# Output projection of a hybrid decoder layer: half of its feature tiles by seven half-size products for eight

## The chip, the cores and the metric

One core of a Trainium2 chip runs the whole layer. The metric is the device time of one execution in microseconds, the median of several runs; a profile is one such execution, and its rows are read with times counted from the start of its span.

## What is computed

A decoder layer on 512 tokens of 2048 features, in fp32. RMS-normed input times a combined weight gives queries, keys, values, gates and gate paths (z) of two head groups: an attention group of 16 heads (NSA, with a branch over compressed blocks of keys and values) and a recurrent group of 8 heads (HGRN2). The parts that matter here:

```python
kc = compress_blocks(k_cmp, pe_k, w1_k, w2_k)      # gelu(blk @ w1) @ w2
vc = compress_blocks(v_cmp, pe_v, w1_v, w2_v)      # the second compression
...
o_a = head_rmsnorm(o_a, nsa_out_norm[l], NSA_HEADS) * jax.nn.silu(z_a)
o_h = head_rmsnorm(o_h, hgrn_out_norm[l], HGRN_HEADS) * jax.nn.silu(z_h)
mixed = jnp.concatenate([o_a, o_h], axis=-1)       # (512, 2048)
x = x + mixed @ w_out[l]                           # w_out: (2048, 2048)
return rmsnorm(x, final_norm)
```

## The kernel before

**Matmuls.** Every large product is done in two-part numbers. An operand is cast to the fp32r type (the high part, on ScalarE) and the rest is subtracted out (the low part, on VectorE); `parts` does so for weights (L315, L316), `split` for transposed activations (L215, L216). A product of 128 features, 128 tokens and 512 columns is then three TensorE matmuls: high by high, low by high, high by low. Weights come by DMA from SyncE's queue (SP) as 128x1024 pieces; the raw piece and its two parts are three of the ten buffers of the pool `w` (`WBUF`).

**Order.** The stages are Python generators; `run` interleaves two of them by the costs that they yield, which gives the order of the program. A list scheduler then lays out each engine's queue: earlier in the program goes first, but what its plan takes to be ready may go ahead. Each engine then works its queue strictly in that order.

**The stages.** First the keys and values to be compressed, then projections of which 12 of 16 feature tiles are already done by seven half-size products for eight (`seven`). Then key and query projections (`make_kd`, `make_q`; 48 matmuls each, L571 to L573) beside the two compressions (`compress`): the first beside query pair 1, the second beside `make_kd(0, 1)` and `make_q(2)`. `blocks` (L623 to L637) builds a compression's input from rows that DMAs bring back, for the second one on GpSimd's queue. The compression's first product is L653 (two passes for each fp32 matmul), its last L682. Then `attention`, interleaved with the remaining key and query projections as filler; then the recurrent heads with further projections as filler.

**Gating.** `gate_chunk(zc, ...)` normalizes four tiles of heads, multiplies by the gate path (L1146, VectorE), transposes on TensorE into the bank `ps_tp` (L1136; there is one such bank) and splits the result (L215 on ScalarE, L216 on VectorE) into the left operand `mT`. Chunks 0 and 1 (attention heads) give feature tiles 0 to 7, chunks 2 and 3 (recurrent heads) tiles 8 to 15. `z_proj` makes the gate paths on TensorE; chunks 1 and 2 run beside its last call.

**Output projection.** Three column chunks of 512 go through `proj_tm` (L596 to L598): for each pair of feature tiles the weights, then four token tiles. Chunk 3 of the gating runs beside the first of them. At the end of a chunk `out_done` adds the residual on VectorE (L1219), squares on ScalarE (L1221) and multiplies by the final norm's gain on GpSimd (L1222). The last column chunk (`last_chunk`, weights loaded ahead by `last_weights`) goes token tile by token tile (L1248 to L1250), so that each finished row can be normalized (L1251 to L1272) and written while the next is multiplied.

**Left over from `seven`:** the list `free_banks` of PSUM bank pairs. When it has been used for the two projections by `seven`, it stands at (lp, lp), (tp, ot), (pj, pj), (pj, pj).

## Time and profile before

| | us |
|---|---|
| median of 3 runs | 1099.39 (1098.72 to 1101.68) |
| the profiled execution | 1101.15 |
| its span in the profile | 1099.4 |
| TensorE busy in it | 1077.6 (98%), mean granted clock 0.995 |
| VectorE busy | 658.2 (60%) |
| ScalarE busy | 419.7 (38%) |
| GpSimd busy | 98.6 (9%) |

PE is TensorE, PEld its weight loads, DVE VectorE, ACT ScalarE, POOL GpSimd, SP SyncE. Matmuls are pipelined: a matmul's time is longer than the distance to the next one's start, and it is the distance that counts for the sum. On VectorE, too, an instruction can start a little before the one ahead of it has ended. The chain of waits is followed back from the last instruction; "busy" says nothing of whether an engine was waited for. A line such as L316 stands for every call of the helper.

### The profile page before, as it was taken

What the parts mean: (1) busy time and instruction counts of PE and PEld (TensorE: products, weight loads), DVE (VectorE), ACT (ScalarE), POOL (GpSimd) and SP (SyncE); (2) the same over time, 40 slices, a digit from 0 to 9 for tenths busy, and PEclk for the clock granted to TensorE, in tenths of its full rate; (3) what the DMA queues carried; (4) which work ended last, traced back from release to release, by engine and by line L of the source; (5) the groups of instructions that cost most, each with busy time, mean ns of one, the idle gap of its engine ahead of it and who ended that gap; (6) DMA issues with size and microseconds to landing.
All of it is one profiled execution on the core that took longest, in us unless ns stands there. A gap on an engine that the chain in (4) does not pass through costs nothing.

```text
span 1099.4 us, 15321 instructions
## 1 busy us (share of the span) xinstructions
PE 1077.6 (98%) x5644; PEld 888.2 (81%) x5644; DVE 658.2 (60%) x1550; ACT 419.7 (38%) x835; POOL 98.6 (9%) x170
## 2 busy tenths in 40 slices
PE   9999999999989999999999999999999999999996
PEld 8799888888868777777877888888887888888886
DVE  4767756764444676576765565666676788424332
ACT  6534433442123565555553222222222443324211
POOL 1000000102431020110200000000000000202010
PEclk9999999999999999999999999999999999999999
DMA  9535346544973322222212323221221723334223
GB/s 311 167 104 172 106 139 212 158 161 140 278 203 96 77 58 58 62 73 58 59 39 78 95 69 106 77 77 58 77 74 48 249 91 106 111 112 167 100 86 125
DMA packets 100011, 127.46 MB, mean 116 GB/s; under 512 B 6672, under 2 KB 62368, under 8 KB 99936
## 3 DMA queue, kind: packets, MB, share of 16 engines
q1 hardware_dynamic: 94368, 113.90, 33.9%
q0 software_dynamic: 2624, 8.39, 2.2%
q10 hardware_dynamic: 2944, 4.19, 1.1%
q8 instruction: 45, 0.74, 0.3%
q14 instruction: 30, 0.25, 0.1%
HBM read 106.01 MB, written 12.06 MB: 107 GB/s over the span
## 4 chain that ended last, share of the span: by engine, by line
PE 91%; DVE 4%; issue 2%; DMA 2%; ACT 1%; SPq 0%; ACTq 0%; POOL 0%; DVEq 0%; POOLq 0%
PE pj L571 9%; PE pj L572 9%; PE pj L573 9%; PE pj L596 7%; PE pj L598 7%; PE pj L597 7%; PE ot L838 4%; PE pj L819 3%; PE lp L987 3%; PE pj L470 2%; PE pj L468 2%; PE pj L469 2%; PE lp L805 2%; PE lp L653 2%; PE lp L806 1%
## 5 line engine op out<-in xcount | busy, mean ns | idle before, releaser
L316 DVE TENSOR_TENSOR w<-w,w 128x1024 fp32r<-128x1024 f32 (+3 forms) x169 | 204.0, 1213 | 180.7 <-ACT w L315 89.3
L315 ACT CAST w<-w 128x1024 fp32r<-128x1024 f32 (+3 forms) x169 | 173.0, 1036 | 273.2 <-DMA w<-in_w_in_dram 150.5
L571 PE MATMUL pj<-hh,w 128*128 128x512 f32 x448 | 183.5, 410 | 0.7 <-ACT pt L828 0.7
L572 PE MATMUL pj<-hl,w 128*128 128x512 f32 x448 | 178.4, 398 | 0.0
L573 PE MATMUL pj<-hh,w 128*128 128x512 f32 x448 | 176.5, 394 | 0.0
L596 PE MATMUL pj<-w,hh 128*128 128x512 f32 (+2 forms) x352 | 127.1, 361 | 0.0
L597 PE MATMUL pj<-w,hl 128*128 128x512 f32 (+2 forms) x352 | 125.9, 358 | 0.0
L598 PE MATMUL pj<-w,hh 128*128 128x512 f32 (+2 forms) x352 | 125.6, 357 | 0.0
L571 PEld LDWEIGHTS pj<-hh,w 128*128 128x128 f32 x448 | 84.3, 188 | 18.5 <-issue 2.9
L573 PEld LDWEIGHTS pj<-hh,w 128*128 128x128 f32 x448 | 84.2, 188 | 17.3 <-issue 0.3
L572 PEld LDWEIGHTS pj<-hl,w 128*128 128x128 f32 x448 | 84.4, 188 | 16.7 <-issue 2.1
L774 DVE CUSTOM_DVE_ANT_0 s<-s,lp 128x128 f32<-128x128 f32 (+3 forms) x128 | 60.5, 483 | 38.4 <-PE lp L806 35.4
L779 ACT ACTIVATE s<-s,mn 128x128 f32<-128x128 f32 (+3 forms) x128 | 71.6, 560 | 28.4 <-DVE mn L774 19.1
L598 PEld LDWEIGHTS pj<-w,hh 128*128 128x128 f32 x352 | 66.4, 189 | 8.5
L596 PEld LDWEIGHTS pj<-w,hh 128*128 128x128 f32 x352 | 66.5, 189 | 8.2
L597 PEld LDWEIGHTS pj<-w,hl 128*128 128x128 f32 x352 | 66.5, 189 | 7.9
L819 PE MATMUL pj<-ident,s 128*128 128x128 f32 x320 | 53.8, 274 | 0.4 <-ACT s L779 0.4
L828 ACT COPY pt<-pj 128x256 f32<-128x256 f32 (+2 forms) x56 | 25.7, 458 | 57.7 <-PE pj L819 57.5
L838 PE MATMUL ot<-pt,s 128*64 128x512 f32 (+3 forms) x256 | 47.3, 440 | 0.0
L819 PEld LDWEIGHTS pj<-ident,s 128*128 128x128 f32 x320 | 39.7, 140 | 9.5 <-ACT s L779 3.0
L838 PEld LDWEIGHTS ot<-pt,s 128*64 128x64 f32 x256 | 22.9, 136 | 21.5 <-issue 11.8
L596 PE MATMUL pj<-w,s 128*128 128x512 f32 x96 | 37.7, 393 | 0.0
(349 smaller groups left out, 1926.2 us busy)
## 6 DMA issues: line engine op xcount, KB each, us to landing
w<-in_w_in_dram SPq DMA_DIRECT2D x121, 512.0 KB, 3.6
w<-in_w_out_dram SPq DMA_DIRECT2D x32, 512.0 KB, 3.5
s<-s SPq DMA_DIRECT2D x48, 128.0 KB, 2.3
w<-in_x_dram SPq DMA_DIRECT2D x16, 256.0 KB, 6.6
d<-e POOLq DMA_DIRECT2D x12, 256.0 KB, 2.4
l<-in_x_dram SPq DMA_DIRECT2D x12, 256.0 KB, 5.2
out_dram<-l SPq DMA_DIRECT2D x12, 256.0 KB, 3.1
w<-in_w_in_dram SPq DMA_DIRECT2D x5, 456.0 KB, 3.2
```

What stands on the lines that cost most here:

```text
L315: nc.scalar.copy(hi, raw)
L316: nc.vector.tensor_tensor(lo, raw, hi.bitcast(FP32), ALU.subtract)
L571: nc.tensor.matmul(acc[j], wh, hh, start=kk == 0, stop=False)
L572: nc.tensor.matmul(acc[j], wh, hl, start=False, stop=False)
L573: nc.tensor.matmul(acc[j], wl, hh, start=False, stop=kk == NK - 1)
L596: nc.tensor.matmul(o, ah, hi[:, k, :], start=kk == 0, stop=False)
L597: nc.tensor.matmul(o, al, hi[:, k, :], start=False, stop=False)
L598: nc.tensor.matmul(o, ah, lo[:, k, :], start=False, stop=kk == NK - 1)
L774: nc.vector.tensor_tensor_reduce(out=y, in0=e["bias"][:, 384 - i * P:512], in1=lp, scale=1.0, scalar=3e38, op0=ALU.add, op1=ALU.min, accum ...
L779: nc.scalar.activation(y, y, AF.Exp, bias=mn, scale=-1.0, accum_out=e["ls"][:, 2 * i + b:2 * i + b + 1])
L819: nc.tensor.transpose(tps[:, j * P:(j + 1) * P], y[:, j * P:(j + 1) * P], ident)
L838: nc.tensor.matmul(e["ot"][b * 64:(b + 1) * 64, j * P:512], v_tok[j][:, b * 256 + g * DH:b * 256 + (g + 1) * DH], e["pt"][:, b, j * 512:38 ...
```

## The change

The output projection is done in two halves of 1024 columns (`out_pair`). In each, feature tiles 0 to 7 (four pairs) are multiplied by a seven-product scheme: the left operand is cut into blocks of 256 tokens by 128 features (A11, A12, A21, A22) and sums of them (S1 to S4), the weights likewise into two blocks of columns and sums of these (`first`, `second`, `third`); two pairs of feature tiles make one step. Tiles 8 to 15 are multiplied as before (`left_out`), into the same banks. The left sums are made by `y_sums` after gating chunk 1, into 12 tiles of the pool `late`, which grows to 21. Corrections from the products go through VectorE (`after_first`, `after_third`) into u2 and u3; GpSimd adds them to the residual (`take_room`), and VectorE adds the bank to that (`out_done`). The first step's products use the bank pairs (lp, lp), (tp, ot) and (pj, pj) in the order A11, S3, S2. In the last column block, tiles 8 to 15 go row by row as before, with their weights kept ready.

The second compression runs beside `make_kd(1, 0)`, which was the first filler of the attention stage; `make_kd(0, 1)` and `make_q(2)` go ahead of it without it.

```diff
--- before.py
+++ after.py
-NLATE = 18
+NLATE = 21
...
+    ysum = []
+    def y_sums(lo, hi):
+        for j in range(lo, hi):
+            pr = [[mT[part][2 * j + r] for part in range(2)] for r in range(2)]
+            a = b4(FP32).rearrange("p (r c) -> p r c", r=2)
+            for r in range(2):
+                nc.vector.tensor_tensor(a[:, r], pr[r][0].bitcast(FP32), pr[r][1].bitcast(FP32), ALU.add)
+            x11, x21, x12, x22 = [a[:, r, h * 256:(h + 1) * 256] for r in range(2) for h in range(2)]
+            t = sl()
+            nc.vector.tensor_tensor(t[:, 0:256], x21, x11, ALU.subtract)
+            nc.vector.tensor_tensor(x22, x21, x22, ALU.add)
+            nc.vector.tensor_tensor(x11, x11, x22, ALU.subtract)
+            nc.vector.tensor_tensor(x12, x12, x11, ALU.add)
+            d2, d14 = late(F32R), [late(F32R), late(F32R)]
+            d2 = [d2[:, 0:256], d2[:, 256:512]]
+            d3 = [pr[0][part][:, 256:512] for part in range(2)]
+            for (h, l), src in ((d3, t[:, 0:256]), (d2, x11), (d14, a[:, 1])):
+                nc.scalar.copy(h, src)
+                nc.vector.tensor_tensor(l, src, h.bitcast(FP32), ALU.subtract)
+            ysum.append({"S2": d2, "S4": [d[:, 0:256] for d in d14], "S1": [d[:, 256:512] for d in d14], "S3": d3,
...
+            yield 0.5
...
-        run((chain(make_kd(0, 1), make_q(2)), 22), (compress(vblk, w1_v, w2_v, False), 22))
-    fill = [make_kd(1, 0), make_q(3), make_kd(1, 1)] + [make_q(p) for p in range(4, 8)]
+        run((chain(make_kd(0, 1), make_q(2)), 22))
+        run((make_kd(1, 0), 11), (compress(vblk, w1_v, w2_v, False), 10))
+    fill = [make_q(3), make_kd(1, 1)] + [make_q(p) for p in range(4, 8)]
...
-        run((attention(), 160), (chain(*fill, hgrn_qf(0)), 113))
+        run((attention(), 160), (chain(*fill, hgrn_qf(0)), 102))
...
-        (chain(gate_chunk(1, o_nsa[4:8], 2, sz[1]), gate_chunk(2, o_h[0:4], 1, sz[2])), 21))
+        (chain(gate_chunk(1, o_nsa[4:8], 2, sz[1]), y_sums(0, 4), gate_chunk(2, o_h[0:4], 1, sz[2])), 23))
...
+    PO = 4
+    wo_half = w_out2.rearrange("(j h p) c -> h p j c", h=2, p=P)
...
+    def take_room(t, c, alloc, u=None):
+        y = alloc()
+        nc.sync.dma_start(out=y, in_=x2[t * P:(t + 1) * P, c * 512:(c + 1) * 512])
+        if u is not None:
+            nc.gpsimd.tensor_tensor(y, y, u, ALU.add)
+        ys[t][c] = y
+    def out_done(t, c, bank):
+        y = ys[t][c]
+        add(y, y, bank)
+        junk = sl()
+        nc.scalar.activation(junk, y, AF.Square, accum_out=yss[:, t, c:c + 1])
+        nc.gpsimd.tensor_tensor(y, y, fns[c], ALU.mult)
+    def left_out(bank, t, k0, w, cs=slice(0, 512)):
+        hi, lo = w
+        for k in range(2):
+            ah, al = [mT[part][k0 + k][:, t * P:(t + 1) * P] for part in range(2)]
...
+    def out_pair(p):
+        c0 = 1024 * p
+        last = p == 1
+        t2 = b8("hl3").rearrange("p (g j c) -> p g j c", g=2, j=2)
...
+        def products(jj, left, bank, fresh, w):
+            hi, lo = w
+            if fresh and jj == 0:
+                banks[bank] = free_banks.pop(0)
+                acc[bank] = [f() for f in banks[bank]]
+            for tt in range(2):
+                ts = slice(tt * P, (tt + 1) * P)
+                for j in range(2):
+                    ah, al = [v[:, ts] for v in ysum[2 * jj + j][left]]
...
+        def first(jj):
+            b11, b22, b12 = load(0, jj, 0), load(1, jj, 1), load(0, jj, 1)
+            w1 = parts(b11)
+            sub(b12, b12, b22)
+            sub(t2[:, jj], b12, b11)
+            return w1, parts(b12), parts(t2[:, jj])
+        def second(jj):
+            b21, t4 = load(1, jj, 0), b4(FP32).rearrange("p (j c) -> p j c", j=2)
+            add(t4, t2[:, jj], b21)
+            return parts(t4), parts(b21)
+        def third(jj):
+            b22 = load(1, jj, 1)
+            add(t2[:, jj], t2[:, jj], b22)
+            return parts(t2[:, jj]), parts(b22)
+        alloc = (lambda: late()) if p == 0 else (lambda: sl())
+        def after_first():
+            u2.extend([sl(), sl()])
+            u3.extend([sl(), sl()])
+            for tt in range(2):
+                nc.scalar.copy(u2[tt], acc["1"][tt])
+            for tt in range(2):
+                add(u2[tt], acc["6"][tt], u2[tt])
+                add(u3[tt], acc["7"][tt], u2[tt])
+            free_banks.extend([banks["6"], banks["7"]])
+            for t in range(NT):
+                take_room(t, 2 * p, late, u3[t - 2] if t > 1 else None)
+        def after_left():
+            for t in range(NT):
+                out_done(t, 2 * p, acc["14"[t // 2]][t % 2])
+            free_banks.extend([banks["4"], banks["1"]])
+            for tt in range(2):
+                take_room(2 + tt, 2 * p + 1, alloc, u3[tt])
+        def after_third():
+            for tt in range(2):
+                add(u2[tt], acc["5"][tt], u2[tt])
+                take_room(tt, 2 * p + 1, alloc, u2[tt])
...
+        for prepare, names, after in (
+                (first, (("A11", "1", True), ("S3", "7", True), ("S2", "6", True)), after_first),
+                (second, (("A22", "4", True), ("A12", "1", False)), None),
+                (third, (("S1", "5", True), ("S4", "3", True)), after_third)):
...
+                    if right and last:
+                        v = b8(("hh2", "hl2", "hh3", "hl3")[n], F32R)
+                        to = v[:, 0:1024], v[:, 1024:2048]
+                    return load_w(w_out2, k0, 2, c0 + 512 * right, 512, to)
...
+        for n in range(len(steps) + 1):
+            if n < len(steps):
+                while steps[n][4] > len(mT[0]):
+                    yield None
+                ready.append(steps[n][0]())
...
-    last_w = []
-    for c in range(3):
...
-        p = proj_tm([], w_out2, mT, c * 512, 512, out_done(c))
-        if c == 0:
-            run((p, 41), (gate_chunk(3, o_h[4:8], 1, sz[3]), 17))
...
-    last_chunk()
+    run((out_pair(0), 82), (gate_chunk(3, o_h[4:8], 1, sz[3]), 42))
+    run((out_pair(1), 1))
```

## Rows read from the trace of the kernel before

**Rows 1.** Chain of waits, shares of the span by engine.
```profile
PE 91%; DVE 4%; issue 2%; DMA 2%; ACT 1%; SPq 0%; ACTq 0%; POOL 0%; DVEq 0%; POOLq 0%
```

**Rows 2.** Windows: length; busy us of PE, PEld, DVE, ACT, POOL; clock; DMA.
```profile
340.00:660.00 320.00, 317.36 (x1733) 246.50 (x1732) 204.13 (x605) 154.31 (x400) 34.02 (x60) 1.00 0.26 71
859.00:942.00 83.00, 82.48 (x394) 67.16 (x393) 71.66 (x212) 35.16 (x50) 0.00 (x0) 1.00 0.39 125
959.00:1045.00 86.00, 86.00 (x381) 71.23 (x380) 30.39 (x32) 26.47 (x36) 10.98 (x9) 1.00 0.39 132
```

**Rows 3.** Timeline of TensorE, 296 to 350 us: start, us, instruction, [idle before].
```profile
299.77 1.95 PE L653 MATMUL lp<-s,w 128*128 128x128 f32 x16
301.47 0.48 PE L571 MATMUL pj<-hh,w 128*128 128x512 f32 x1
...
327.11 10.30 PE L653 MATMUL lp<-s,w 128*128 128x128 f32 x64 [5.36 <-issue]
337.16 0.47 PE L571 MATMUL pj<-hh,w 128*128 128x512 f32 x1
...
348.74 0.39 PE L573 MATMUL pj<-hh,w 128*128 128x512 f32 x1
```

**Rows 4.** Windows of TensorE: length, busy, granted clock, DMA.
```profile
330.00:331.00 1.00, 1.00 (x7) 0.50 0.00 0
```

**Rows 5.** Timeline of ScalarE, then of VectorE, 258 to 350 us.
```profile
310.26 1.05 ACT L315 CAST w<-w 128x1024 fp32r<-128x1024 f32 x1
322.57 1.04 ACT L315 CAST w<-w 128x1024 fp32r<-128x1024 f32 x1 [11.26 <-DMA w<-in_w_in_dram]
...
324.79 3.83 DVE L637 TENSOR_TENSOR s<-s,col 128x124 f32<-128x124 f32 x14
```

**Rows 6.** Timeline of TensorE in the output projection.
```profile
911.83 0.39 PE L596 MATMUL pj<-w,s 128*128 128x512 f32 x1
...
912.64 0.48 PE L598 MATMUL pj<-w,s 128*128 128x512 f32 x1
...
958.76 0.39 PE L596 MATMUL pj<-w,s 128*128 128x512 f32 x1
...
959.45 0.39 PE L596 MATMUL pj<-w,s 128*128 128x512 f32 x1
```

**Rows 7.** Timeline of VectorE from 835 to 962 us.
```profile
845.12 0.42 DVE L966 TENSOR_TENSOR s<-s,s 128x256 f32<-128x256 f32 x1 [1.22 <-PE tp L1032]
...
903.77 0.69 DVE L1158 SCALAR_TENSOR_TENSOR s<-s,pj 128x512 f32<-128x512 f32 x1
904.37 0.17 DVE L143 TENSOR_SCALAR roi<-roa 128x16 int32<-128x16 int32 x1
...
907.46 1.23 DVE L316 TENSOR_TENSOR w<-w,w 128x1024 fp32r<-128x1024 f32 x1
908.60 0.17 DVE L151 TENSOR_TENSOR roi<-roi,rot 128x16 f32<-128x16 f32 x1
...
953.22 1.49 DVE L316 TENSOR_TENSOR w<-w,w 128x1024 fp32r<-128x1024 f32 x1 [1.73 <-ACT w L315]
```

**Rows 8.** Groups of VectorE, 859 to 942 us: count, busy, mean ns, idle before.
```profile
L316 DVE TENSOR_TENSOR w<-w,w 128x1024 fp32r<-128x1024 f32 x13 | 15.9, 1222 | 0.6 <-ACT w L315 0.6
...
L216 DVE SCALAR_TENSOR_TENSOR hl<-tp,col,hh 128x512 fp32r<-128x512 f32 x8 | 6.0, 750 | 5.6 <-ACT hh L215 5.5
```

**Rows 9.** Groups of GpSimd over the whole span.
```profile
L1222 POOL TENSOR_TENSOR l<-l,s 128x512 f32<-128x512 f32 x12 | 17.9, 1495 | 199.6 <-ACT s L1221 199.6
```

**Rows 10.** Timeline of VectorE, 1040 to 1100 us.
```profile
1078.64 0.69 DVE L1251 TENSOR_TENSOR s<-s,pj 128x512 f32<-128x512 f32 x1 [6.10 <-PE pj L1250]
...
1082.62 0.75 DVE L1268 SCALAR_TENSOR_TENSOR s<-s,la,s 128x512 f32<-128x512 f32 x1
```

**Rows 11.** Timeline of ScalarE, 930 to 950 us.
```profile
933.48 0.69 ACT L215 ACTIVATE hh<-tp,col 128x512 fp32r<-128x512 f32 x1 [4.32 <-PE tp L1136]
...
938.05 0.69 ACT L215 ACTIVATE hh<-tp,col 128x512 fp32r<-128x512 f32 x1 [2.95 <-PE tp L1136]
```

More of the change, by code (lines that the diff above doesn't have):

```diff
@@ L1213, in hymba_layer @@
     fns = []
-    def out_done(c):
-        def done(t, acc):
-            y = late()
-            nc.sync.dma_start(out=y, in_=x2[t * P:(t + 1) * P, c * 512:(c + 1) * 512])
-            nc.vector.tensor_tensor(y, y, acc, ALU.add)
-            junk = sl()
-            nc.scalar.activation(junk, y, AF.Square, accum_out=yss[:, t, c:c + 1])
-            nc.gpsimd.tensor_tensor(y, y, fns[c], ALU.mult)
-            ys[t][c] = y
-        return done
-    def last_weights(lo, hi):
-        for i in range(lo, hi):
-            if i < 4:
-                if i % 2 == 0:
-                    pair = b8(f"hh{2 + i // 2}", F32R), b8(f"hl{2 + i // 2}", F32R)
-                wt = [a[:, (i % 2) * 1024:(i % 2 + 1) * 1024] for a in pair]
-            else:
-                wt = None
-            last_w.append(load_w(w_out2, 2 * i, 2, 1536, 512, wt))
-            yield 1.0
@@ new lines, in finish_row @@
+    def finish_row(t, pre, a):
+        last = 4 if t == NT - 1 else 3
+        v, g, u = [a[:, i:i + 1] for i in range(3)]
+        nc.vector.tensor_scalar(v, yss[:, t, last:last + 1], 1.0 / D, pre, ALU.mult, ALU.add)
+        nc.vector.tensor_scalar(g.bitcast(I32), v.bitcast(I32), 1, None, ALU.logical_shift_right)
+        nc.vector.tensor_scalar(g.bitcast(I32), g.bitcast(I32), -1, 0x5F3759DF, ALU.mult, ALU.add)
+        nc.vector.tensor_scalar(v, v, -0.5, None, ALU.mult)
+        for _ in range(3):
+            nc.vector.scalar_tensor_tensor(u, g, g, v, ALU.mult, ALU.mult)
+            nc.vector.scalar_tensor_tensor(g, u, 1.5, g, ALU.add, ALU.mult)
+        for c in (1, 0, 2, 3):
+            y = ys[t][c]
+            if c == 3:
+                nc.vector.scalar_tensor_tensor(y, y, g, fns[3], ALU.mult, ALU.mult)
+            elif c == 1:
+                nc.vector.tensor_scalar(y, y, g, None, ALU.mult)
+            else:
+                nc.scalar.mul(y, y, g)
+            nc.sync.dma_start(out=out2[t * P:(t + 1) * P, c * 512:(c + 1) * 512], in_=y)
@@ L1238, in last_chunk @@
         for t in range(NT):
[L1239 to L1241 removed]
+            bank = acc["35"[t // 2]][t % 2]
+            y, junk = ys[t][3], sl()
             a, pre = sm(3, "la"), sm(1, "lp")
[L1243 to L1251 removed]
+            halves_ = (slice(0, 256), slice(256, 512)) if t == NT - 1 else (slice(0, 512),)
@@ L1252, in last_chunk @@
+            for h, cs in enumerate(halves_):
+                for k0 in range(2 * PO, NK, 2):
+                    left_out(bank, t, k0, w_ready[k0], cs)
+                nc.vector.tensor_tensor(y[:, cs], y[:, cs], bank[:, cs], ALU.add)
                 nc.scalar.activation(junk[:, cs], y[:, cs], AF.Square, accum_out=yss[:, t, 3 + h:4 + h])
-                last = 3 + h
-            nc.vector.tensor_reduce(pre, yss[:, t, 0:last], AX.X, ALU.add)
+            nc.vector.tensor_reduce(pre, yss[:, t, 0:2 + len(halves_)], AX.X, ALU.add)
```

103 lines of the change are left out of this document (60 added, 43 removed).

## Prediction

> **What bounds the kernel now.** I read the chain of waits first: nine tenths of what ends last is TensorE, so time comes off only by fewer matmuls or fewer stalls [rows 1]. The windows by stage say where another engine is close behind. In the output projection's later columns VectorE works 30 of 86 us under a TensorE that never pauses. In the stage just before and at its start (859 to 942 us, gating beside the last z projection), VectorE works 71.7 of 83 us and TensorE still pauses only 0.5 us [rows 2]. What the change adds there lands on an engine with 11 us to spare, which is the first thing to hold on to.
>
> Then the list of TensorE's idle times, which has one large entry: 5.36 us ahead of the second compression's matmuls, at 327 us [rows 3]. The stretch after it runs at a granted clock of 0.50, the lower level of 1.2 GHz [rows 4]. The same 16 passes of the first compression take 1.70 us at the full clock (299.77 to 301.47), so 64 take 6.8 us; here they took 10.05 us [rows 3]. The stall costs 5.4 us and the clock after it 3.25 us: 8.6 us together.
>
> **Part A, the compression moved.** TensorE stands still because its queue has those 64 passes next and their input is late. Fourteen of the sixteen VectorE ops that build the input run only from 324.79 to 328.6 us, when DMAs from GpSimd's queue have landed [rows 5]. Behind the waiting passes stood work that could run: 42 of the 48 matmuls of query pair 2 (337.16 to 348.74, with the compression's last small matmuls between) [rows 3], whose weights were cast at 310.26 and 322.57 us [rows 5]. With the compression queued after them, TensorE goes on from 321.6 to 331.1 us (42 x 0.227). The input is complete by then, and the passes stand among matmuls of the key projection moved out of the attention stage. That projection brings its two weight loads, casts and subtractions, and its eight key copies on SP's queue with it; they pass the second compression's loads, and the same number leaves the attention stage. I take the whole 8.6 us; the bounds are 0 (the same late input, or weights delayed by the loads it shares the queues with) and 8.6.
>
> The price: attention loses 48 of its filler matmuls. There TensorE was idle 2.6 of 320 us [rows 2], with projections filling the waits on VectorE and ScalarE. The filler shrinks by a tenth, so the waits may show: nothing as the one end, and as the other 3 us, about a doubling of that idle. I take 1.5.
>
> **Part B, fewer matmuls.** Four pairs of feature tiles, two column halves: for 1024 columns, 4 x 8 x 3 x 2 = 192 products become 7 x 2 x 4 x 3 = 168. All have the same shape, 128x128 by 128x512. Over both halves 48 go. Three products start 0.69 us after the three before (958.76 to 959.45), 0.227 each over longer stretches [rows 6]: **10.9 us** of TensorE.
>
> **What VectorE gets for it.** I use the distance from one start to the next. That is 1.14 us for a 128x1024 subtraction (907.46 to 908.60; it is 1.23 long), 0.60 for an op on 128x512 (903.77 to 904.37), and for 128x256, 0.42 long, 0.34 by the same overlap of 0.08 [rows 7].
> - The sums of the left side: for each pair three ops on 512 and six on 256, 3.9 us, times four 15.5 us. They stand between gating chunks 1 and 2.
> - The three-product steps: five ops on 1024, twice, 11.4 us; the next two-product steps three, twice, 6.8 us.
> - The corrections after the first step: four PSUM adds, 2.4 us.
> - The weights of four left-out pairs of the left column block: 4.6 us.
>
> That is 40.7 us, all due before the left column block is complete. VectorE's 71.7 us in 859 to 942 hold 13 weight subtractions, six of them, from 907.46 us on, the output projection's (7.3 us at 1.22 each) [rows 2, 8]. Without those, 64.4 us of gating and z work stay; with the new work 105.1. Without a pause VectorE is done at 964.1 us. TensorE would want the last of it at 911.8 + 192 x 0.227 (72 + 48 + 72 products ahead of the last left-out pair) + 2.9 for eight sets of transposes = 958.2. (One set put 0.36 us between products: 911.83 to 912.64 where two steps of 0.227 were due.) [rows 6] So TensorE is held 5.9 us if VectorE never pauses. In 859 to 942 the second halves of chunks 2 and 3's splits alone waited 5.6 us for ScalarE and TensorE [rows 8]; all of that again makes 11.5. Since VectorE now has more ready work for such pauses I take 8.5.
>
> ScalarE gets casts for all this, but works 35 of 83 us there [rows 2]. DMA grows by 4 loads of 512 KB to 36 at a busy share of 0.39; hidden, unless a load waits for a buffer.
>
> **The residual on GpSimd.** VectorE's add of the bank stays, so nothing is taken from it. GpSimd gets 12 adds of 1.5 us [rows 9], each due a product step or more later; in the tight stretch there are two. One VectorE subtraction, among GpSimd's multiplications at 953 us, took 1.49 us where others take 1.22 to 1.23 [rows 7, 8]: 0.5 us for two, inside the 8.5.
> The Trainium skill (SBUF — State Buffer, "Who interferes with whom") has it harder: a VectorE instruction with two SBUF inputs and a GpSimd one that reads SBUF exclude each other for the whole instruction. By that rule the two adds could hold VectorE 3 us, and the sum below would be 2.5 us higher; the trace shows a lengthening of 0.26 us only, so the sum goes by the row.
>
> **Later columns and tail.** The right block and the second column half ask VectorE for 6.8 + 2.4 + 1.2 + 4.6 us over some 33 us of TensorE, and for 11.4 + 6.8 + 4.8 over 27. There is room. At the joints the ten weight buffers (nine in a three-product step) can delay a load: 0 to 2 us, I take 1. At the end a row comes every 5.4 us and not every 10.9; its VectorE chain takes 4.7 us (1078.64 to 1083.37) [rows 10]. It fits: 0.
>
> **Sum.** -8.6 + 1.5 - 10.9 + 8.5 + 1.0 = -8.5 us. The profiled execution took 1101.15 us (span 1099.4 and 1.75 around it): 1092.65. It was one of the slower ones; from the median of 1099.39 the sum gives 1090.9. I say **1092 us**.
>
> **Rivals.**
> 1. VectorE does not hold TensorE. Its pauses before 942 us swallow the sums, or products that need no gate run ahead. For it: 11.3 us of pauses [rows 2], and the first product uses gated tiles directly, no sums. Against: 40.7 us of new work on top, for 11.3 us of pauses. Lateness 0: -17.0, 1084 from the profiled execution, 1082 from the median.
> 2. The gates' transposes queue behind the products (slower). The product with S3 holds the bank that the transposes use, from its first matmul until VectorE's corrections. The eight transposes of chunks 2 and 3 then follow one by one, each waiting for ScalarE and VectorE to empty the bank. If that is 939 us (911.8 + 16.3 + 2.4 + the 8.5) and each takes 4.6 us, as where TensorE mixed them with products (933.48 to 938.05) [rows 11], the last is ready at 975.8 and TensorE 17 us late. A pause so long brings the lower clock, 3.25 us by the stall of today: 20.3 in place of 8.5, +3.3, 1104 from the profiled execution. It decides from 17.0 us on, where all gains are used up. Against: at 2.4 us each they cost nothing (939 + 8 x 2.4 = 958).
> 3. The compression still waits, the move does nothing: part A 0 (or +1.5), the whole about -1.4 to 0.1: 1100 from the profiled execution, 1098.5 from the median. For it: the input's DMAs and GpSimd's queue order stay as they were. Against: the 42 matmuls whose weights were there.
>
> **Chances.** The forecast 0.46 (its own range 1087 to 1098, from lateness 5.9 to 11.5, joints, filler and the two starting times), rival 1 0.18, rival 2 0.18, rival 3 0.18. The range 1083 to 1104 reaches to rivals 1 and 2. A difference under 0.3% (3.3 us) counts as none. Faster: 0.40 of the forecast, all of rival 1, 0.04 of rival 3: 0.62. Slower: most of rival 2, a little of the rest: 0.16. Same: 0.22.
>
> **What the profile after will show.** Part A: no idle over 1 us and no clock under full between 318 and 340 us. Part B: 720 products in the output projection in place of 768. The lateness: idle of TensorE between its first output product and the end of the left block, released by VectorE, 6 to 12 us, with VectorE over 90% busy. Past it, under 2 us idle until the end. Wrong would be a TensorE idle there that names the transposes' bank, or pauses in the later columns named for DMA or GpSimd.

## The result and the profile after

The changed kernel takes **1126.65 us** (median of 4, 1125.49 to 1128.22) against 1099.22 of the kernel before in the same session (1098.72 to 1101.68): ratio **1.0255**, 95% interval 1.0236 to 1.0273. The forecast was 1092 with a range to 1104: wrong in sign. The profiled execution took 1125.49 us, its span 1123.8 against 1099.4.

Windows of the kernel after (columns as in [rows 2]): the place of the old stall, two stretches of [rows 2], then two windows of 20 us:

```profile
320.00:340.00 20.00, 20.00 (x108) 17.18 (x107) 11.25 (x22) 5.45 (x6) 0.18 (x2) 1.00 0.87 243
...
859.00:942.00 83.00, 65.45 (x281) 51.01 (x279) 75.01 (x217) 31.82 (x50) 0.00 (x0) 0.86 0.33 105
959.00:1045.00 86.00, 79.08 (x347) 63.57 (x345) 50.25 (x44) 29.85 (x43) 21.00 (x13) 1.00 0.40 129
...
880.00:900.00 20.00, 10.00 (x37) 6.90 (x36) 19.09 (x68) 6.91 (x13) 0.00 (x0) 0.72 0.11 38
900.00:920.00 20.00, 13.16 (x48) 10.11 (x48) 17.88 (x52) 7.27 (x13) 0.00 (x0) 0.68 0.11 35
```

The old stall is gone (first line, clock 1.00). In its place TensorE loses 17.5 of the 83 us from 859 to 942, where it lost 0.5 [rows 2], and over that whole stretch VectorE is not full: 75.0 of 83. From 880 to 920 us, in the middle of it, VectorE is nearly full (19.1 and 17.9 of 20) and TensorE idle for 10.0 and 6.8 of 20. Past 959 us, where TensorE never paused before, it now loses 6.9 of 86 us.

The timeline of TensorE after, the lines with the longest waits and three landmarks:

```profile
886.59 0.66 PE L1136 MATMUL tp<-ident,s 128*128 128x128 f32 x4 [1.90 <-DVE s L216]
888.81 1.12 PE L1136 MATMUL tp<-ident,s 128*128 128x128 f32 x4 [1.57 <-DVE s L216]
891.49 1.12 PE L1136 MATMUL tp<-ident,s 128*128 128x128 f32 x4 [1.56 <-DVE s L216]
897.44 0.79 PE L596 MATMUL pj<-w,hh 128*128 128x512 f32 x1 [4.83 <-ACT w L315]
898.03 0.63 PE L597 MATMUL pj<-w,hl 128*128 128x512 f32 x1
898.46 0.63 PE L596 MATMUL pj<-w,hh 128*128 128x512 f32 x1
...
908.06 0.79 PE L598 MATMUL pj<-w,hh 128*128 128x512 f32 x1 [6.84 <-DVE w L316]
...
932.30 0.39 PE L1314 MATMUL lp<-w,s 128*128 128x512 f32 x1
...
1037.58 0.50 PE L1314 MATMUL lp<-w,s 128*128 128x512 f32 x1 [1.67 <-ACT w L315]
...
1113.96 0.28 PE L1268 MATMUL pj<-hl,hh 128*128 128x256 f32 x1
```

Five waits, 16.7 us together, stand ahead of the output projection, in the last z projection: three sets of transposes and two products (L596, L598) whose weights are not yet cast (L315) or subtracted (L316). The lower clock comes with them: after 897 us a product starts every 0.43 us and not every 0.227. The first output product starts at 932.30 instead of 911.83 [rows 6].

The whole difference of the spans, by landmarks: the last recurrent matmul (L1077) starts 4.0 us earlier (848.4 against 852.4); from there to the first output product +24.5; from there to the last matmul (1089.84 before, 1113.96 now) +3.65, which is 10.9 fewer for 48 matmuls and 14.5 more for waits and joints; the tail +0.3. That makes +24.4.

What stood in front of the late weights, from the timelines of VectorE and ScalarE after:

```profile
862.79 1.23 DVE L316 TENSOR_TENSOR w<-w,w 128x1024 fp32r<-128x1024 f32 x1
...
905.60 0.68 DVE L1183 TENSOR_TENSOR l<-w,l 128x512 fp32r<-128x512 f32 x1
...
906.79 1.22 DVE L316 TENSOR_TENSOR w<-w,w 128x1024 fp32r<-128x1024 f32 x1
...
895.83 0.62 ACT L1182 CAST l<-w 128x512 fp32r<-128x512 f32 x1 [0.27 <-DVE w L1177]
896.35 1.04 ACT L315 CAST w<-w 128x1024 fp32r<-128x1024 f32 x1
```

For 44 us, 862.79 to 906.79, VectorE subtracts no weight at all. In the last 15 of them it works without a pause, for the most part on the sums of the left operand (L1171 to L1183); ScalarE's casts of the z weights stand behind the sums' casts in the same way. Buffers change too: the sums' scratch takes four of the ten weight buffers, and the last two loads of z weights are asked for at 897.43 and 906.31 us, where the kernel before asked at 877.76 and 880.28. e2 and e3 below separate the two.

### The profile page after: what moved, and what is told of

Read it like the earlier page. It is cut to its first block, busy times and chain, and to the rows that moved or that the text cites. A ratio compares the mean times of both kernels' runs of the same rounds, so it can differ in the third digit from the quotient of the medians.

```text
span 1123.8 us, 15299 instructions
## 1 busy us (share of the span) xinstructions
PE 1078.4 (96%) x5572; PEld 879.0 (78%) x5572; DVE 724.4 (64%) x1626; ACT 439.3 (39%) x863; POOL 122.6 (11%) x182
## 4 chain that ended last, share of the span: by engine, by line
PE 51%; DVE 9%; issue 3%; ACT 2%; DMA 1%; POOL 0%; ACTq 0%; POOLq 0%; SPq 0%; DVEq 0%
PE pj L571 6%; PE pj L572 6%; PE pj L573 6%; PE ot L838 4%; PE pj L819 3%; PE lp L987 3%; PE pj L598 2%; PE pj L596 2%; PE pj L597 2%; DVE w L316 2%; PE lp L805 2%; PE lp L806 1%; PE pj L1266 1%; PE pj L1268 1%; PE pj L1267 1%
## 5 line engine op out<-in xcount | busy, mean ns | idle before, releaser
L316 DVE TENSOR_TENSOR w<-w,w 128x1024 fp32r<-128x1024 f32 (+3 forms) x173 | 212.0, 1234 | 157.6 <-ACT w L315 91.0
L315 ACT CAST w<-w 128x1024 fp32r<-128x1024 f32 (+3 forms) x173 | 176.6, 1037 | 266.7 <-DMA w<-in_w_in_dram 146.7
L572 PE MATMUL pj<-hl,w 128*128 128x512 f32 x448 | 178.0, 397 | 0.0
L572 PEld LDWEIGHTS pj<-hl,w 128*128 128x128 f32 x448 | 84.4, 188 | 15.7 <-issue 1.0
L596 PE MATMUL pj<-w,hh 128*128 128x512 f32 (+2 forms) x256 | 91.3, 357 | 4.8 <-ACT w L315 4.8
L598 PE MATMUL pj<-w,hh 128*128 128x512 f32 (+2 forms) x256 | 88.8, 349 | 6.8 <-DVE w L316 6.8
L597 PE MATMUL pj<-w,hl 128*128 128x512 f32 (+2 forms) x256 | 89.9, 351 | 0.0
L598 PEld LDWEIGHTS pj<-w,hh 128*128 128x128 f32 x256 | 49.2, 192 | 12.5 <-DVE w L316 7.6
L596 PEld LDWEIGHTS pj<-w,hh 128*128 128x128 f32 x256 | 49.4, 193 | 9.9 <-ACT w L315 5.2
L597 PEld LDWEIGHTS pj<-w,hl 128*128 128x128 f32 x256 | 49.4, 193 | 4.7
L838 PE MATMUL ot<-pt,s 128*64 128x512 f32 (+3 forms) x256 | 50.3, 441 | 0.8 <-DVE pt L830 0.8
L838 PEld LDWEIGHTS ot<-pt,s 128*64 128x64 f32 x256 | 24.4, 136 | 21.4 <-issue 9.7
L987 PE MATMUL lp<-s,s 128*128 128x192 f32 x192 | 35.9, 330 | 0.5 <-POOL s L1002 0.2
```

What stands on the lines that cost most here:

```text
L315: nc.scalar.copy(hi, raw)
L316: nc.vector.tensor_tensor(lo, raw, hi.bitcast(FP32), ALU.subtract)
L572: nc.tensor.matmul(acc[j], wh, hl, start=False, stop=False)
L596: nc.tensor.matmul(o, ah, hi[:, k, :], start=kk == 0, stop=False)
L597: nc.tensor.matmul(o, al, hi[:, k, :], start=False, stop=False)
L598: nc.tensor.matmul(o, ah, lo[:, k, :], start=False, stop=kk == NK - 1)
```

## The experiments

Each run is compared with runs of the kernel before on the same chip; ratios are to those.

### The sums: what and where

**e13_sums_alone.** The kernel before, plus the sums:

```diff
-        (chain(gate_chunk(1, o_nsa[4:8], 2, sz[1]), gate_chunk(2, o_h[0:4], 1, sz[2])), 21))
+        (chain(gate_chunk(1, o_nsa[4:8], 2, sz[1]), y_sums(0, 4), gate_chunk(2, o_h[0:4], 1, sz[2])), 23))
... (y_sums and its tiles as in the change, but for)
+            d3 = [t[:, 256:512].bitcast(F32R), t[:, 0:256].bitcast(F32R)]
```

> The kernel before with one thing added: the sums of the left operand, computed where the changed kernel computes them, into tiles that nothing reads. Slack theory (the prediction's: VectorE has 11.3 us of pauses in this stage, and only work beyond them costs): 15.5 less 11.3, so 3 to 6 us more than the kernel before, and no single wait over 2 us. Order theory (VectorE's queue is in order, and the sums stand ahead of the subtractions of the z projection's later weights, whatever pauses come afterwards): waits of z products on those weights of 3 us and more each at the place where the changed kernel has its 4.8 and 6.8, with a lower granted clock beside them, and 10 to 25 us more than the kernel before.

Measured 1123.38 us, ratio 1.0204 (1.0178 to 1.0231): 22 us for 15.5 us of VectorE work. The timeline of TensorE and a window of this kernel:

```profile
886.61 1.00 PE L1136 MATMUL tp<-ident,s 128*128 128x128 f32 x4 [1.90 <-DVE s L216]
889.18 1.11 PE L1136 MATMUL tp<-ident,s 128*128 128x128 f32 x4 [1.56 <-DVE s L216]
891.86 1.11 PE L1136 MATMUL tp<-ident,s 128*128 128x128 f32 x4 [1.56 <-DVE s L216]
897.80 0.80 PE L596 MATMUL pj<-w,hh 128*128 128x512 f32 x1 [4.83 <-ACT w L315]
908.42 0.80 PE L598 MATMUL pj<-w,hh 128*128 128x512 f32 x1 [6.84 <-DVE w L316]
```

```profile
880.00:900.00 20.00, 10.01 (x36) 6.84 (x35) 18.84 (x67) 6.62 (x12) 0.00 (x0) 0.67 0.11 28
```

The same five waits, to a hundredth of a microsecond, with no seven products anywhere. From the last recurrent matmul (848.4) to the last matmul (1109.76) it takes 23.9 us longer than before; 16.7 are the five waits, and the remaining 7.2 I put to the lower clock of the matmuls between them. Of these 4.5 can be read off: the 21 products that start from 897.80 to 900.96 and from 908.42 to 913.7 us take 9.3 us, where 0.227 each makes 4.8. The slack theory falls. This run does not tell the order of the queues from the buffers that the scratch holds.

Why the slack was not there shows in the windows of the kernel before, cut smaller than in [rows 2]:

```profile
860.00:880.00 20.00, 19.75 (x95) 15.75 (x94) 18.96 (x61) 8.49 (x14) 0.00 (x0) 1.00 0.66 211
880.00:900.00 20.00, 20.00 (x98) 16.48 (x97) 16.83 (x59) 6.46 (x11) 0.00 (x0) 1.00 0.26 87
900.00:920.00 20.00, 19.72 (x95) 15.98 (x94) 19.52 (x53) 12.70 (x20) 0.00 (x0) 1.00 0.32 98
920.00:940.00 20.00, 20.00 (x97) 16.48 (x96) 13.66 (x39) 4.88 (x6) 0.00 (x0) 1.00 0.30 103
```

Of the 11.3 us of VectorE's pauses only 4.7 lie between 860 and 920 us (60 less 18.96, 16.83 and 19.52), where the sums and the z weights are due; 6.3 lie in the 20 us after. Fifteen and a half on 4.7 is 10.8 late; the two products waited 11.7. That the two figures are near each other supports the reading and does not prove it.

**e2_sums_last** puts the sums behind gating chunk 2, **e3_own_buffers** keeps them in place and takes their scratch from two large tiles instead of the weight pool:

```diff
--- e2
-        (chain(gate_chunk(1, o_nsa[4:8], 2, sz[1]), y_sums(0, 4), gate_chunk(2, o_h[0:4], 1, sz[2])), 23))
+        (chain(gate_chunk(1, o_nsa[4:8], 2, sz[1]), gate_chunk(2, o_h[0:4], 1, sz[2]), y_sums(0, 4)), 23))
--- e3
-            a = b4(FP32).rearrange("p (r c) -> p r c", r=2)
+            if j % 2 == 0:
+                ya = b8(f"h{'hl'[j // 2]}1")
+            a = ya[:, (j % 2) * WCOLS:(j % 2 + 1) * WCOLS].rearrange("p (r c) -> p r c", r=2)
```

> The changed kernel with the left sums made after gating chunk 2 and not ahead of it. Theory buffers (the four 128x1024 pieces of the sums hold four of the ten weight buffers for some 30 us, so the z projection's weights can't be loaded and cast): the z projection's weights go ahead, and 15 to 20 of the 24.5 us lost between the recurrent heads and the first output product come back; 1107 to 1112 us. Theory work (VectorE has 15.5 us more to do there, whatever the order): TensorE then waits ahead of its first or second output product for the sums, and at most 10 us come back; 1117 us or more.

> The changed kernel with the sums' four pieces in a room of their own, the parts of the normed input that the last z projection has finished with, and not in the pool of the weights; the order of the program is as in the changed kernel. Theory buffers: the z projection's weights are cast and subtracted in time, 15 us or more of the 24.5 come back; 1106 to 1112 us. Theory work: the sums still stand ahead of the weights in the queues of ScalarE and VectorE; less than 8 us come back; 1119 us or more.

Measured: e2 1122.12 us, 1.0196 (1.0162 to 1.0229); e3 1125.52, 1.0235 (1.0197 to 1.0273). A window of e2 and a line of its TensorE's timeline, then the same of e3:

```profile
920.00:940.00 20.00, 13.76 (x47) 9.81 (x48) 19.45 (x44) 9.44 (x15) 0.00 (x0) 0.81 0.43 140
```

```profile
922.97 0.80 PE L1314 MATMUL lp<-w,s 128*128 128x512 f32 x1 [4.16 <-ACT w L315]
```

```profile
900.00:920.00 20.00, 10.99 (x41) 8.12 (x40) 19.35 (x59) 10.27 (x20) 0.00 (x0) 0.74 0.00 0
```

```profile
913.71 0.80 PE L598 MATMUL pj<-w,hh 128*128 128x512 f32 x1 [8.66 <-DVE w L316]
```

In both the waits at 886 to 908 us are gone and others come from 905 us on: in e2 at transposes and the output projection's weights, in e3 still at the z weights. In both VectorE is busy 19.2 us of 20 and more from 880 to 960. Both times the work theory's forecast held. So the place of the sums is worth some 6 us by the ratios, and the weight pool nothing that can be measured (the intervals of e3 and the changed kernel overlap): buffers decide where TensorE waits, but with the sums in it, the queue ahead of the left block is full wherever they stand.

**e8_no_sums** leaves the sums out (the products read plain blocks in their place), **e7_sums_gpsimd** has GpSimd do their adds and subtractions:

```diff
--- e8: the nine VectorE operations and three casts of a pair go
-            a = b4(FP32).rearrange("p (r c) -> p r c", r=2)
...
+            ysum.append({"S2": [v[:, 256:512] for v in pr[0]], "S4": [v[:, 0:256] for v in pr[1]],
+                         "S1": [v[:, 256:512] for v in pr[1]], "S3": [v[:, 256:512] for v in pr[0]],
--- e7: six of the nine
-                nc.vector.tensor_tensor(a[:, r], pr[r][0].bitcast(FP32), pr[r][1].bitcast(FP32), ALU.add)
+                nc.gpsimd.tensor_tensor(a[:, r], pr[r][0].bitcast(FP32), pr[r][1].bitcast(FP32), ALU.add)
...
```

> The changed kernel without the sums of the left operand: the products read plain blocks in their place, so the first output columns are wrong numbers; all matmuls, weights' sums and joints stand. Work theory: VectorE has 15.5 us less to do between 860 and 960 us and the span falls by that much or a little more, 1105 to 1111. Rival (the waits come from the weight buffers, or from the order of a step's casts, or at the joints of the seven products): 1115 to 1125, with waits of the products on the weights' casts at the places where they stand in the changed kernel.

> The changed kernel with the adds and subtractions of the left operand's sums on GpSimd; VectorE keeps the casts. Work theory (each us of VectorE between 860 and 960 is a us of the span): about 10 us of VectorE's work leave that stretch, so 1114 to 1119. Rival (GpSimd takes longer for the same tiles, and the products wait for its sums instead): no faster than the changed kernel, 1124 to 1135.

Measured: e8 1111.40 us, 1.0084 (1.0060 to 1.0107); e7 1134.29, 1.0298 (1.0278 to 1.0318). Taking the 15.5 us of work away gives back 1.7% of 1100, some 19 us; the median is 0.4 us above the work theory's range and below the rival's. Giving it to GpSimd is worse than leaving it. From e7, GpSimd's first add, and the wait of TensorE:

```profile
870.26 1.32 POOL L1171 TENSOR_TENSOR w<-s,s 128x512 f32<-128x512 f32 x1 [40.01 <-DVE s L216]
...
914.31 0.79 PE L596 MATMUL pj<-w,hh 128*128 128x512 f32 x1 [16.11 <-ACT w L315]
```

An add that takes VectorE 0.69 takes GpSimd 1.32, and the z product waits 16.1 us in one piece.

e8 also shows what is left without sums: 190.2 us from its first output product to its last matmul (909.9 to 1100.07) against 178.0 before, with 10.9 us of matmuls fewer, so 23 us of other losses. A window of e8:

```profile
909.90:1100.00 190.10, 173.41 (x775) 139.61 (x775) 127.06 (x188) 67.39 (x97) 42.16 (x24) 0.98 0.36 115
```

Of the 23 us 16.7 are idle time of TensorE, 9.8 of that before the left block is complete at 976.5 us.

**e6_gate3_late** is e2 with gating chunk 3 behind the second step, so that VectorE comes to that step's weights first:

```diff
-    run((out_pair(0), 82), (gate_chunk(3, o_h[4:8], 1, sz[3]), 42))
+    pair0 = out_pair(0)
+    run((upto(pair0, 26.9), 1))
+    run((pair0, 55), (gate_chunk(3, o_h[4:8], 1, sz[3]), 15))
```

The final norm's tiles are loaded in `after_left` for it, since the slabs that chunk 3 holds are needed.

> The kernel e2_sums_last with the gating of row chunk 3 put behind the second step of the output projection, and the slabs of the final norm loaded after the left half, so that there is room for it. Order theory (what VectorE does ahead of the second step's weights decides: about 12 us of gating stand before them, while TensorE still has some 120 products after them that could cover that gating): the second step's waits shrink by about 10 us, 1110 to 1114. Rival (VectorE is full from 880 to 960 us and only its sum of work counts, so that the left block is complete when VectorE is, in whatever order): within 3 us of e2_sums_last, 1119 to 1125.

Measured 1119.29 us, 1.0156 (1.0139 to 1.0173): some 4 us less than e2 by the ratios, but the two intervals overlap, and the median lies in the rival's range (1119 to 1125). The 10 us of the order theory are not there; whether this order counts at all is not shown. Up to 920 us it stalls as e2 does, and after that its products wait for ScalarE's casts of the steps' weights (the longest 4.16 and 2.28 us) while VectorE is no longer full (15.7 of 20 us from 920 to 940).

### The joints of the seven products

In the second half of the changed kernel the second three-product step and the step after it wait 1.67, 1.63 and 0.58 us. SyncE, VectorE and ScalarE ahead of the first of these:

```profile
1025.03 1.41 SPq L1301 DMA_DIRECT2D w<-in_w_out_dram  x3
...
1032.85 1.23 DVE L1245 TENSOR_TENSOR w<-w,w 128x1024 f32<-128x1024 f32 x1 [1.08 <-DMA w<-in_w_out_dram]
...
1035.09 0.59 ACT L1342 COPY s<-pj 128x512 f32<-128x512 f32 x1 [4.59 <-PE pj L1316]
...
1036.48 1.05 ACT L315 CAST w<-w 128x1024 fp32r<-128x1024 f32 x1
```

Three pieces are asked for at once at 1025.03, when buffers come free, and the last has landed 7.8 us later. ScalarE's cast then stands behind two copies for the corrections that wait for TensorE. Two theories, buffers or queue order. **e9_raw_apart** loads the raw pieces into large tiles that stand empty then:

```diff
+        r11, r22, r12 = [b8(t).rearrange("p (g j c) -> p g j c", g=2, j=2) for t in ("hh2", "hl2", "hh3")]
...
-            b11, b22, b12 = load(0, jj, 0), load(1, jj, 1), load(0, jj, 1)
+            b11, b22, b12 = load(0, jj, 0, r11[:, jj]), load(1, jj, 1, r22[:, jj]), load(0, jj, 1, r12[:, jj])
```

> The changed kernel with the six raw weight pieces of the two three-product steps loaded into three large tiles that stand empty then, so that a three-product step takes six of the ten weight buffers and not nine. Buffer theory of the joints (the waits after 987 us, about 6 us in all, come because the next step's loads wait for the buffers of the step before, and three loads of 512 KB then take some 8 us): 3 to 5 us of the 6 go, 1121 to 1124, and the waits of the products on the casts at 1037, 1045 and 1047 us of the changed kernel are gone; ahead of 960 us little changes, since VectorE is full there. Rival (ScalarE's order: a cast stands behind a copy that waits for a product): the waits stay, 1125 to 1128.

Measured 1133.75 us, 1.0297 (1.0275 to 1.0319): slower than the changed kernel, and above the ranges of both theories. The joints of the second half did go (windows from 1020 to 1100 without a pause), but the first half paid for it. SyncE, VectorE and TensorE of e9 there:

```profile
934.28 0.38 SPq L1303 DMA_DIRECT2D hh<-in_w_out_dram  x1
...
939.33 1.23 DVE L1245 TENSOR_TENSOR hh<-hh,hl 128x1024 f32<-128x1024 f32 x1 [2.97 <-issue]
...
956.46 1.23 DVE L1245 TENSOR_TENSOR hh<-hh,hl 128x1024 f32<-128x1024 f32 x1 [3.16 <-DMA hh<-in_w_out_dram]
...
941.69 0.79 PE L1316 MATMUL tp<-w,s 128*128 128x512 f32 x1 [4.70 <-ACT w L315]
```

The large tiles hold the input that the z projection still reads, so the last pieces of the two three-product steps are asked for only at 934.28 and 935.69 us (in the kernel after, the first step's three at 919 us); to these I put the 2.97 us that VectorE, with no time to give, stands still. The subtraction at 956.46 is the fifth of its line (L1245), and a half has four: it belongs to the second half. The free tiles let the plan bring it forward into the full stretch, where VectorE stands still 3.16 us for its input.

### The second compression

**e1_move_only** is the kernel before with the moved compression alone, **e4_no_move** the changed kernel without it.

```diff
--- e1, from the kernel before (e4, from the kernel after, has it the other way round)
-        run((chain(make_kd(0, 1), make_q(2)), 22), (compress(vblk, w1_v, w2_v, False), 22))
+        run((chain(make_kd(0, 1), make_q(2)), 22))
+        run((make_kd(1, 0), 11), (compress(vblk, w1_v, w2_v, False), 10))
```

> The kernel before with the second compression's move alone; the output projection is as before. Theory 1 (the attention stage gives back most of the gain, as in the changed kernel's trace: its recurrent heads end at 848.4 us against 852.4): 3 to 5 us faster than before, 1094.5 to 1096. Theory 2 (the move is worth the whole stall and clock loss of 8.6 us less 1.5, and the 4 us were an effect of the output projection's plan on earlier queues): 6 to 9 us faster. Both: no TensorE idle of 5 us at 320 to 340 us.

> The changed kernel with the second compression where it was before. If the two parts add: the output projection's part alone costs the 27.4 us of the whole and the 4 us that the move saves, so 1130 to 1132 us. If the earlier stages' end changes how the sums and the z projection meet: it departs from that by more than 3 us either way.

Measured: e1 1099.19 us, 0.9988 (0.9970 to 1.0007), no difference; e4 1132.82, 1.0292 (1.0258 to 1.0325), 0.4% above the changed kernel, and the two intervals overlap. Neither of e1's theories (3 to 5 us and 6 to 9 us faster) held. **e5_half_query** keeps the order before and lets the compression start only beside the second half of query pair 2; the attention keeps all its filler:

```diff
-  run((chain(make_kd(0, 1), make_q(2)), 22), (compress(vblk, w1_v, w2_v, False), 22))
+  q2_gen = make_q(2)
+  run((chain(make_kd(0, 1), upto(q2_gen, 5.0)), 16))
+  run((q2_gen, 5), (compress(vblk, w1_v, w2_v, False), 8))
```

> The kernel before, with one move only: the second compression starts beside the second half of the first query product instead of beside the whole key product of chunk 1, and no work is taken from what the attention has beside it. Theory 1 (moving the key product ahead of the attention cost the attention its cover, which is why e1_move_only kept only 2.5 of 8.6 us): the stall of 5.4 us and the slower clock of that stretch go and nothing is given back, so 6 to 8.6 us less than before, 1091 to 1093.5. Theory 2 (the attention is set by its own chain of VectorE and ScalarE and takes up any lead that TensorE brings into it): 1 to 2.5 us less than before, as e1_move_only, with the attention's last product at most 3 us earlier than in the kernel before. Theory 3 (the casts' way is too long for half of a query product): the stall stands in part, 2 to 4 us of it.

Measured 1096.87 us, 0.9951 (0.9934 to 0.9969): 5.4 us less, short of theory 1's 6 and far over theory 2's 2.5. The start of the attention (L791) and its last products (L838) in e1, then in e5:

```profile
349.15 0.29 PE L791 MATMUL lp<-kw,s 128*128 128x288 f32 x1
...
L838 PE MATMUL ot<-pt,s x16: 272/432/643, 588.0 to 592.7; 128*64 128x512 f32 x4, 128*64 128x384 f32 x4, 128*64 128x256 f32 x4, 128*64 128x128 f32 x4
```

```profile
340.71 0.40 PE L791 MATMUL lp<-kw,s 128*128 128x288 f32 x1 [1.04 <-ACT s L659]
...
L838 PE MATMUL ot<-pt,s x16: 272/432/643, 586.9 to 589.0; 128*64 128x512 f32 x4, 128*64 128x384 f32 x4, 128*64 128x256 f32 x4, 128*64 128x128 f32 x4
```

The attention takes 248.3 us in e5 and 243.5 in e1, 246.2 before (348.97 to 595.2). With 48 matmuls (10.9 us) fewer beside it, it is 2.7 us shorter: what TensorE had done ahead came back as 8.2 us of time that no list of waits names. The attention begins 8.3 us earlier in e5 and ends 6.2 earlier; in e1 it begins 0.2 later and ends 2.5 earlier. That a chain of VectorE and ScalarE paces it fits this, but no run shows it.

### Seven products where VectorE has room

**e10_second_half** computes the first half as before, makes the sums beside column chunk 1, and has e5's compression; **e11_second_half_raw** adds the raw pieces in large tiles. In both, the sums overwrite parts of the left operand that column chunk 1 still reads, so its columns come from other numbers; instructions and sizes are the same. **e14_second_half_right** gives these parts a tile of their own:

```diff
--- all three
-    run((out_pair(0), 82), (gate_chunk(3, o_h[4:8], 1, sz[3]), 42))
+    for c in range(2):
...
+        p = proj_tm([], w_out2, mT, c * 512, 512, plain_done(c))
+        run((p, 41), (gate_chunk(3, o_h[4:8], 1, sz[3]), 17) if c == 0 else (y_sums(0, 4), 4))
     run((out_pair(1), 1))
--- e14
+                d3s.append(b8("hh3", F32R).rearrange("p (j h c) -> p j h c", j=4, h=2))
+            d3 = [d3s[0][:, j, part] for part in range(2)]
...
+        r11, r22 = [b8(t).rearrange("p (g j c) -> p g j c", g=2, j=2) for t in ("hh2", "hl2")]
```

> The seven products in the second column half alone; the first half is computed as in the kernel before, the sums of the left operand stand beside column chunk 1, where VectorE has room, and the second compression starts beside half a query product, as in e5_half_query. Work theory (VectorE is the bound only because the new work lands on the stretch of gating): no stall before 1000 us, 24 products fewer (5.4 us), less the joints' waits of the second half, 4 to 6 us in the changed kernel: within 1.5 us of e5_half_query, that is 5 to 7 us less than the kernel before. Rival (the seven products cost more than they save wherever they stand): 3 us or more above e5_half_query. If the joints' waits too came from VectorE's backlog, 10 to 11 us less than the kernel before.

> e10_second_half with the raw pieces of the three-product steps in the large empty tiles. Buffer theory of the joints: 2 to 4 us less than e10_second_half, so 8 to 10 us less than the kernel before and faster than every kernel so far. Rival (ScalarE's order): the same as e10_second_half within 1 us.

> e11_second_half_raw with the third pieces of the sums in a large tile of their own (there and in e10_second_half they overwrote a quarter of the left-hand tiles that the products of column chunk 1 were still to read, so that those columns differed from the reference), and with two of the three kinds of raw pieces in large tiles, not three. Work theory: the products of chunk 1 no longer wait for the sums (1.0 us in e11_second_half_raw), the joints stay without a wait over 1 us: 1093 to 1096, 6 to 9 us less than the kernel before. Rival (the third raw piece in the weight buffers brings the joints' waits back): 1097 to 1100, as e10_second_half.

Measured: e10 1099.87 us, 0.9988 (0.9976 to 1.0001); e11 1095.57, 0.9948 (0.9928 to 0.9968); e14 **1093.94**, 0.9941 (0.9921 to 0.9961). Windows of e14, its last recurrent matmul (846.5) and its last matmul:

```profile
859.00:942.00 83.00, 81.99 (x390) 66.58 (x389) 67.42 (x200) 32.87 (x46) 0.00 (x0) 1.00 0.39 124
985.00:1065.00 80.00, 79.78 (x352) 65.51 (x351) 51.84 (x48) 28.34 (x39) 22.32 (x14) 1.00 0.37 119
```

```profile
L1077 PE MATMUL ot<-s,s x48: 271/275/377, 639.2 to 846.5; 128*128 128x128 f32 x48
```

```profile
1082.79 0.28 PE L1271 MATMUL pj<-hl,hh 128*128 128x256 f32 x1
```

No stall in the gating stage, and a second half in which TensorE pauses 0.2 of 80 us. e10 against e11 settles the joints where VectorE is not late: the same products with the raw pieces in the weight pool cost 4.3 us more, with waits of 0.5 to 1.1 us at the same joints. So buffers, not ScalarE's order. e10 by itself came out as its rival said, 4 us above e5; e11 and e14 show that the joints made that loss. e11 misses its 8 to 10 us (5.7), e14 is inside its 6 to 9 (6.5 by the ratio). e14 is faster than both kernels; against e5 alone (0.9951) its interval does not tell it apart, although its span is 1092.2 against 1095.3. Most of what it has on the kernel before is e5's compression: of the 2.7 us that its last matmul is ahead of e5's (1085.52), 1.5 are there at the last recurrent matmul (848.0 in e5), ahead of the output projection. So no run shows that the seven products by themselves save time; where VectorE has room they cost none.

**e12_all_mended** has seven products in both halves with e6's order, e9's raw pieces and e5's compression:

```diff
+        r11, r22, r12 = [b8(t).rearrange("p (g j c) -> p g j c", g=2, j=2) for t in ("hh2", "hl2", "hh3")]
...
+    run((pair0, 55), (gate_chunk(3, o_h[4:8], 1, sz[3]), 15))
...
+        run((q2_gen, 5), (compress(vblk, w1_v, w2_v, False), 8))
```

> The seven products in both halves with all that has helped: the sums after the third gating chunk and the fourth behind the second step (e6_gate3_late), the raw pieces in the large tiles, the second compression beside half a query product. Work theory: VectorE still has some 40 us more to do before the left block is complete, so TensorE still waits there for about what e6_gate3_late shows, less the part that came from weight buffers: 1108 to 1114, slower than the kernel before. Rival (the waits there come mainly from the nine buffers of a three-product step): 1098 to 1104, no slower than the kernel before.

Measured 1113.15 us, 1.0111 (1.0090 to 1.0132), as the work theory said: still slower than before.

## Why the prediction was wrong

**The step that failed** is the one ("What VectorE gets for it") that put all of VectorE's 40.7 us of new work against one deadline: "all due before the left column block is complete", done at 964.1, wanted at 958.2, so 5.9 to 11.5 late. The sum of work was right, the deadline was not the first one. The sums stand in an in-order queue ahead of the z projection's last weights, which TensorE wants from about 885 us on. There the pauses are 4.7 us and not 11.3. That cost 23.9 us by itself (e13), 7.2 of them put to the lower clock, for which the 8.5 had no entry. In its own place, between the first output product and the end of the left block (932.3 to 990.4), the lateness came out as 5.4 us of idle time, with VectorE busy 28.9 of the first 29.7 us: near the low end of 5.9 to 11.5, but on top of the 24.5 ahead of it. One sum up to one deadline fails without the sums of the left side as well: by it VectorE would then be done at 948.6 (954.2 with all the 5.6 of waits), ahead of 958.2, and e8 still idles 9.8 us before its left block is complete. The loss ahead of the first output product alone, 24.5 us, is more than the 20.3 of rival 2; the mechanism is that rival's only in part. Transposes do follow one by one, each waiting until VectorE's split (L216) has emptied their bank, but for 5.0 of the 16.7 us and ahead of the first product, when no product holds that bank; behind it one set waits 2.17 us (961.76). Rival 1 (no hold) fell too, and so did its "for": the pauses were counted over a stage, not up to a due date. Rival 3 fell too: the compression did not wait.

**Part A.** The stall and its clock went, as foretold. Two terms were mis-sized. The price of the lost filler, taken as 1.5 (0 to 3), was 8.2 (e1): a TensorE idle of 2.6 in 320 us had been read as "TensorE sets the pace", but the attention kept its 243 to 248 us whatever stood beside it. And the 8.6 us are those of one execution: in the trace of e13, whose code is the same up to the z stage, the stall is 2.3 us and the 64 passes run at the full clock (in e4 it is 5.32 us again):

```profile
324.61 7.38 PE L653 MATMUL lp<-s,w 128*128 128x128 f32 x64 [2.32 <-issue]
```

The landmark "4.0 us earlier" at 848 us in the kernel after is therefore no proof for part A: e13, without it, reaches that point at the same 848.4.

**The matmuls.** 48 fewer at 0.227 is 10.9 us. The kernel after runs 720 products where there were 768, as foretold, but no run shows the time whole. In e14 24 are gone (5.4 us), with room for VectorE; from the last recurrent matmul to the last matmul it takes 236.3 us against 237.5 in e5, so 1.2 us came through, 2.5 us went to TensorE's waits in the output projection, and 1.0 us was lost ahead of it.

**Joints**, taken as 1.0 (0 to 2): TensorE's idle in the windows from 980 to 1114 us is 6.9 us in the kernel after. The prediction named the cause (nine of ten buffers) and gave it too little: three loads at once take 7.8 us to land, and the three-product step beside them lasts 8.2 us (36 products at 0.227), which leaves nothing for the two subtractions of 1.23 us and the casts that follow.

**The residual on GpSimd** was taken as 0.5, with a dearer reading 2.5 us above; the dearer one was the better (last section). The row read for it, 1.49 us at 953.22, overlapped GpSimd's multiplication (952.33 to 953.63) for 0.4 us alone. In the tight stretch four adds ran and not two (955.93 to 962.18), and one VectorE operation among them (L1244 at 958.74) took 2.30 us in place of 1.22. **The tail** was nothing, as said (+0.3).

**Left open:** in what parts the 23 us that remain without the sums (e8) are VectorE's queue, ScalarE's queue and late loads in the first half. e6 and e9 changed the time by a few microseconds, one down and one up, and neither was run with the sums out. Nor was e13 run with e3's scratch, which would part queue order from buffers in the loss that the sums make by themselves.

## What to carry to other kernels

Count an engine's free time up to the due date of each thing in its queue, in windows of 20 us, not over a stage: 11 us of pauses were 5 where they were needed. When new work goes to an engine that is nearly full beside TensorE, first add that work alone, unused, and time it: here that one run lost 22 us, the whole change 27. And a TensorE that shows hardly any idle time may still be filling time that a chain elsewhere dictates: taking 10.9 us of work out beside it gave back 2.7 here, starting it 8.3 us sooner ended it 6.2 sooner.

## What the hardware showed

**Waits can cost twice.** With the five waits of 1.6 to 6.8 us, 16.7 together, the granted clock fell to 0.50 (1.2 GHz); by 918 us it was back at 1.00. Windows of the kernel after:

```profile
888.00:897.00 9.00, 2.23 (x8) 1.43 (x8) 8.51 (x24) 3.62 (x7) 0.00 (x0) 0.54 0.00 0
898.00:900.00 2.00, 2.00 (x6) 1.57 (x5) 2.00 (x7) 0.98 (x3) 0.00 (x0) 0.50 0.72 217
...
918.00:922.00 4.00, 4.00 (x22) 3.31 (x21) 1.98 (x2) 1.63 (x2) 0.00 (x0) 1.00 0.47 159
```

In e13 I put 7.2 us to the clock, on 16.7 of waiting. In the kernel after, the scattered later waits, of up to 2.17 us, left the clock at 1.00 (the window 959 to 1045 above).

**GpSimd beside VectorE.** The same VectorE subtraction takes 2.31 us beside GpSimd's residual adds, which take 2.27 each there, and 1.21 when they are over (at 1093.02). VectorE, then GpSimd, in the kernel after:

```profile
1089.57 2.31 DVE L316 TENSOR_TENSOR hl<-w,hl 128x1024 fp32r<-128x1024 f32 x1
1094.03 1.21 DVE L316 TENSOR_TENSOR hl<-w,hl 128x1024 fp32r<-128x1024 f32 x1
...
1083.96 9.06 POOL L1252 TENSOR_TENSOR s<-s,s 128x512 f32<-128x512 f32 x4
```

Not every one is lengthened: one that started at 1088.43, together with an add, took 1.21, and it was the add that took 2.27. In the kernel before the longest such subtraction in the whole span took 1.77. The Trainium skill (SBUF — State Buffer, "Who interferes with whom") says that a VectorE instruction with two SBUF inputs contends with a GpSimd instruction that reads SBUF, as an exclusive lock. The lengthening by 1.1 us agrees with that, better than the 0.26 us that the prediction went by.
